# Early loads and own tiles for the first recurrence, four tiles for the last gates, and a 128 byte shift in a hybrid block kernel

## The chip, the core and the metric

The kernel runs on one core of a Trainium2 chip. The metric is the time of one execution in device microseconds (us); lower is better. Before the change it is 1393.91 us, the median of three runs (1393.51 to 1395.18).

## What is computed

One layer of a streaming encoder block works on 512 tokens of 2048 channels in float32. The normalised input is projected once, and the projection is split into parts:

- Branch A, a gated linear recurrence (HGRN2) with 8 heads of 128: `f = lb + (1 - lb) * sigmoid(a_f)`, `k = 1 - f`, `q = silu(a_q) / sqrt(128)`, and per head the state `S = diag(f) S + k v^T`, output `q S`. The output is normalised per head and multiplied by `silu(a_g)`.
- Branch B, sparse attention: an indexer scores all keys for every query and keeps the best 128, attention over these carries a relative position bias, and the output is multiplied by `silu(b_g)`.
- Merge: `sigmoid(m_a) * (y_a @ w_pa) + sigmoid(m_b) * (y_b @ w_pb)`, then `x + merged @ w_out`, then a last normalisation.

## The kernel before

**Products.** Every large product is made of three TensorE (PE) matmuls on operands split into a high and a low part (`split`, lines 71 to 73; `mm3`, line 75). Weights come from HBM in pieces of 512 KB through SyncE's (SP's) DMA queue into two raw buffers (`load`), are split by ScalarE (ACT) and VectorE (DVE) into one of three pairs `wh`, `wl` (`prep`, up to two pieces ahead), and are used by PE. SP issues in program order: a load that waits for its buffer holds up every DMA that was written behind it.

**Order.** `jobs` is a list of closures that is built by hand and run once. Inside a product job `pump()` is called at fixed places. A pump issues loads, sends out what the two `late` lists hold (stores, two pumps after they were noted) and lets each lane go one step. Lanes are generators: `hgrn` (the recurrences), `top` (the choice of keys), `att` (attention), `norm`, `misc`, `t5` (the bias table). So a lane's instructions stand in each engine's order between the blocks of a product.

**Stages**, in the order of time:

1. Start and first products (to 125 us).
2. Twelve pair units (125 to 584 us) make the gates and, first of all, `a_q` and `a_f` of heads 6 and 7 (stored in DRAM as `qf_d`; the gates as `gate_d`; `ckv_d` was stored before). A pair unit (`pair_unit`, line 1034) is a two by two product with seven multiplications (`PRODUCTS`, line 1024): 8 rounds of 7 x 2 x 3 = 42 matmuls with 256 moving columns. Stationary are the weights, split in pool `pairs` as `bh`, `bl` (three of the seven) and, as sums, in `wh`, `wl` (four of the seven); moving are the input `xh`, `xl` and its sums `sh`, `sl` in pool `sums`.
3. `close_pairs` frees these pools, `open_branches` (line 433) opens `values`, `shared` and `idx` and loads two small constants, and eight jobs of the indexer follow (584 to 645 us).
4. `end_index` (line 1130) frees the indexer's pools, opens `hgrn` (`R.h`) and `norms` (`R.i`), loads `ckv` and starts three lanes: the first recurrence `hgrn_gen(3)` (heads 6 and 7), `t5_gen` and `norm_gen`. Then `ai_job(3)` (line 650) makes the values `v` of these heads: 16 blocks of 12 matmuls with 256 moving columns, moving `wh`, `wl`, stationary `xh`, `xl`. For pair 3 it pumps after blocks 1, 2 and 3 of every four (12 pumps), for the others after 1 and 3 (8 pumps).
5. `af_aq(0)`, `open_att`, `ai_job(1)`, `af_aq(1)`, `ai_job(2)`, `uqkv(0)`, `af_aq(2)`, `uqkv(1)`: the other pairs' recurrence inputs, recurrences 0 to 2, attention.
6. `gate_job(44)` (line 1088) makes the last four gates with 512 moving columns, then `uqkv(2)`, the `w_pa` products and `uqkv(3)`.
7. `open_merge` (line 1217), the `w_pb` products and `merge_pair` (to 1221 us).
8. `out_job`: three pair units over `w_out` (1221 to 1340 us), this time with the merged tokens stationary (`mh`, `ml`, and their sums `so`) and the weights moving (`bh`, `bl` in a new pool `pairs` on the right side; `wh`, `wl`), then the last block and the final normalisation.

**The first recurrence.** `hgrn_gen(3)` loads `f` and `q` from `qf_d` into tiles of `R.h` in its first step (lines 701 to 703) and a gate (line 707); the second step makes `f`, `k` and `q` (lines 714 to 718); eight steps follow, one for each level `l`: `scores(l)` (small matmuls, tile `hl`), then `decay(l)` on DVE and POOL, which the next level's matmuls wait for. The others (`p` 0 to 2) find `f`, `k`, `q` in tiles that `af_evac` and `aq_evac` filled. `af_evac(p)` first runs to its end whatever is left of the recurrence before (`drain("hgrn")`), since the tiles `hf`, `hk` are shared.

**The last gates.** `gate_job` evicts four PSUM tiles with ACT into `gs`, a tile with two buffers in pool `values`, and each is stored to `gate_d` (lines 1090 to 1092).

**Places.** Pools are stacked from both ends of a partition, so a tile's first byte follows from the sizes. What matters below is that byte modulo 256. In the first twelve units: moving `xh` at 36,512, 52,896, ... and the sums from 106,144 on, all 160, apart from the sums of round 2 (`EVEN`), which a 64 byte gap puts at 224; stationary `bh` from 180,192 on and `wh` at 10,400 + 64, all 224. In the three units of `out_job`: moving `bh` from 208,864 on, 224, and `wh` at 10,400 + 192, which is 96 (in round 2 at 10,400, which is 160); stationary `mh` from 106,144 on and `so` at 52,896 and others, all 160. In `ai_job`: moving `wh` 96, stationary `xh` 160.

Of the kernel before, what the change touches and what calls it, by code (L numbers as in the profile page):

```python
# [26 lines left out]
F32 = mybir.dt.float32  # L27
FR = mybir.dt.float32r
AF = mybir.ActivationFunctionType
OP = mybir.AluOpType  # L30
# [4 lines left out]
T, D = 512, 2048  # L35
# [15 lines left out]
def hybrid_block(ctx, tc, x, norm_w, w_in, lb_table, gnorm_a, q_norm_w, kv_norm_w, w_uq,  # L51
# [3 lines left out]
    V, A, G, PE, SP = nc.vector, nc.scalar, nc.gpsimd, nc.tensor, nc.sync  # L55
# [45 lines left out]
    ckv_d = dram.tile([2, 128, T], F32, name="ckv_d")  # L101
    cq_d = dram.tile([4, 128, T], F32, name="cq_d")
    qf_d = dram.tile([2, 2, 128, T], F32, name="qf_d")
# [4 lines left out]
    def enter(name, side=None, space=None):  # L108
        cm = tc.tile_pool(name=name, bufs=1, side=side, reuse_waits="tile")
        pools[name] = (cm, cm.__enter__())  # L110
        return pools[name][1]
# [4 lines left out]
    R = SimpleNamespace()  # L116
# [83 lines left out]
    def drain(name):  # L200
        lane = lanes[name]
        while lane:
            for _ in lane[0]:
                pass
            lane.popleft()

    jobs, hg = [], {}
# [225 lines left out]
    def open_branches():  # L433
        R.v = enter("values")
        R.s = enter("shared")
        R.q = enter("idx", side="right")
        R.M = R.s.tile([128, 1280], F32, name="M")
        R.ckh = R.s.tile([128, 2, T], FR, name="ckh")
        R.ckl = R.s.tile([128, 2, T], FR, name="ckl")
        R.ident = R.s.tile([128, 128], F32, name="ident")  # L440
        R.levels = R.s.tile([128, 6, 32], U8, name="levels")
        SP.dma_start(R.ident, c_ident)
        lev = R.q.tile([128, 6, 32], F32, name="lev", tag="bf")
        SP.dma_start(lev, c_levels.rearrange("p (l t) -> p l t", l=6))
        G.tensor_copy(R.levels, lev)

    def t5_gen():
        rb = R.i.tile([128, H], F32, name="rb")
# [198 lines left out]

    def ai_job(p, places=(1, 3)):  # L650
        at = len(specs)
        c0 = 2048 + p * 256
        for k in range(0, NK, 4):
            specs.append(([(0, 256, w_in[k * 128:(k + 4) * 128, c0:c0 + 256])], 4, 256, MOVED))

        def run():
            ps = [mmp.tile([128, T], F32, name="acc") for _ in range(2)]
            for i in range(4):
                prep(at + i)
                wh, wl = halves.pop(at + i)  # L660
                for k in range(4):
                    kk = i * 4 + k
                    rh, rl = x_rhs(kk)
                    for t in range(4):
                        s = slice(t * 128, t * 128 + 128)
                        mm3(ps[t // 2][:, (t % 2) * 256:(t % 2) * 256 + 256], rh[:, s], rl[:, s],
                            wh[:, k, :], wl[:, k, :], kk == 0 and t % 2 == 0, kk == NK - 1)
                    if k in places:
                        pump()
            v = hg[p, "v"] = R.v.tile([128, 4, 256], F32, name="hv", bufs=2)  # L670
            for i in range(2):
                A.activation(v[:, 2 * i:2 * i + 2, :], ps[i].rearrange("p (t n) -> p t n", t=2), AF.Copy)

        jobs.append(run)

    def af_evac(p):
        def evac(c, ps):
            if c == 0:
                drain("hgrn")
                hg[p, "f"] = R.h.tile([128, 2, T], F32, name="hf")  # L680
                hg[p, "k"] = R.h.tile([128, 2, T], F32, name="hk")
            f, k, h = hg[p, "f"][:, c, :], hg[p, "k"][:, c, :], 2 * p + c
            A.activation(f, ps, AF.Sigmoid)
            V.tensor_scalar(f, f, oml[:, h:h + 1], lb[:, h:h + 1], op0=OP.mult, op1=OP.add)
            V.tensor_scalar(k, f, -1.0, 1.0, op0=OP.mult, op1=OP.add)
        return evac
# [10 lines left out]
        return evac  # L697

    def hgrn_gen(p):
        if p == 3:  # L700
            f, k, q = (R.h.tile([128, 2, T], F32, name=n) for n in ("hf", "hk", "hq"))
            SP.dma_start(f, qf_d[1].rearrange("f p t -> p f t"))
            SP.dma_start(q, qf_d[0].rearrange("f p t -> p f t"))
        else:
            q, k, f = hg[p, "q"], hg[p, "k"], hg[p, "f"]
        gate = R.h.tile([128, 2, T], F32, name="hg")
        SP.dma_start(gate, gate_d[2 * p:2 * p + 2].rearrange("f p t -> p f t"))
        S = R.h.tile([128, 8, 128], F32, name="hS")
# [1 line left out]
        G.memset(near, 0.0)  # L710
        G.memset(S, 0.0)
        qf, kf, tot = (a.rearrange("p c t -> p (c t)") for a in (q, k, f))
        yield
        if p == 3:
            for c in range(2):
                V.tensor_scalar(f[:, c], f[:, c], oml[:, 6 + c:7 + c], lb[:, 6 + c:7 + c], op0=OP.mult, op1=OP.add)
                V.tensor_scalar(k[:, c], f[:, c], -1.0, 1.0, op0=OP.mult, op1=OP.add)
            A.activation(q, q, AF.Copy, scale=128 ** -0.5)
            yield

        def scores(l, ps):

# [60 lines left out]
                                       tot[:, c * 4 + j:c * 4 + j + 1],  # L783
                                       pp[:, j * 128:(j + 1) * 128], op0=OP.mult, op1=OP.add)
        yield
        sq = R.h.tile([128, 2, T], F32, name="hk")
        zs = []
        o = R.h.tile([128, 2, T], F32, name="ho", tag="hf")
        for c in range(2):
            po = bank("ho")  # L790
            for j in range(4):
                sl = slice(j * 128, (j + 1) * 128)
                mm(po[:, sl], v[:, j, c * 128:(c + 1) * 128], S[:, 4 * c + j, :], j == 0, j == 0)
                if j:
                    mm(po[:, sl], st[:, c, j - 1, :], q[:, c, sl], False, True)
            A.activation(o[:, c], po, AF.Copy)
            A.activation(sq[:, c], po, AF.Square)
            yield
            zs.append((R.h.tile([128, T], FR, name="hzh", tag=("hkd", "hst")[c]),
                       R.h.tile([128, T], FR, name="hzl", tag=("hq", "hS")[c])))  # L800
            split(*zs[c], sq[:, c])
        yield
        for c in range(2):
# [8 lines left out]
            V.tensor_tensor(r, r, gate[:, c], op=OP.mult)  # L812
        yield
        for c in range(2):
            y = [R.h.tile([128, T], FR, name=f"hy{i}", tag=(("hkd", "hst"), ("hq", "hS"))[i][c]) for i in range(2)]
            split(*y, sq[:, c])
            for i in range(2):
                late[1].append(lambda y=y[i], i=i, h=2 * p + c: SP.dma_start(ya_d[i, h], y.bitcast(F32)))
# [268 lines left out]

    def gate_job(j0, after):
        def evac(c, ps):
            g = R.v.tile([128, T], F32, name="gs", bufs=2)  # L1090
            A.activation(g, ps, AF.Sigmoid)
            late[1].append(lambda: SP.dma_start(gate_d[j0 + c], g))

        feat_job(w_in, GATE_COL[j0], 4, NK, 2, x_rhs, evac, after=after)
# [35 lines left out]
    def end_index():  # L1130
        lanes["misc"].append(waiting.pop())
        drain("misc")
        leave("idx")
        leave("raws")
        R.h = enter("hgrn", side="right")
        R.i = enter("norms")
        R.ckv = R.i.tile([128, 2, T], F32, name="ckv")
        SP.dma_start(R.ckv, ckv_d.rearrange("f p t -> p f t"))
        lanes["hgrn"].append(hgrn_gen(3))
        lanes["t5"].append(t5_gen())  # L1140
        lanes["norm"].append(norm_gen(R.ckv, 2, c_kvw, R.ckh, R.ckl))
# [11 lines left out]
    def uqkv(p):  # L1153
        feat_job(w_uq, p * 256, 2, 4, 4, c_rhs, uq_evac(p), place=RANK,
                 before=None if p else (lambda: drain("top")))
        ukv_job(p)

    jobs.append(end_index)
    ai_job(3, (1, 2, 3))
    lane("top", top_gen)  # L1160
    af_aq(0)
    jobs.append(open_att)
    ai_job(1)
    af_aq(1)
    ai_job(2)
    uqkv(0)
    af_aq(2)
    uqkv(1)
# [127 lines left out]
    def out_job():  # L1296
# [7 lines left out]
        def run():  # L1304
# [3 lines left out]
            def block_evac(c0):  # L1308
                def evac(ps):
                    p1, p2, p6, p7, p5, p3, p4 = ps  # L1310
                    c = R.v0.tile([128, 4, 256], F32, name="hv")
                    one, u2 = c[:, 0:2, :], c[:, 2:4, :]
                    u3 = R.g.tile([128, 2, 256], F32, name="u3")

                    def part(t0, f0, in0, in1, op):
                        V.tensor_tensor(two[t0 // 2][:, :, c0 + f0:c0 + f0 + 256], in0, in1, op=op)

                    A.activation(one, p1, AF.Copy)
                    V.tensor_tensor(u2, p6, one, op=OP.add)
                    part(0, 256, p2, one, OP.add)  # L1320
                    V.tensor_tensor(u3, p7, u2, op=OP.add)
                    V.tensor_tensor(u2, p5, u2, op=OP.subtract)
                    part(2, 0, p5, u3, OP.subtract)
                    part(0, 0, p3, u2, OP.add)
                    part(2, 256, p4, u3, OP.add)
                return evac
# [83 lines left out]
            for t in range(4):  # L1410
# [16 lines left out]
                o, f = os[t], out2[t * 128:(t + 1) * 128]  # L1427
# [67 lines left out]
```

## Time and profile before

| what | us |
|---|---|
| median of three runs | 1393.91 |
| the profiled execution | 1394.53 |
| its span, first to last instruction | 1392.7 |
| PE busy | 1363.5 (98%) |
| DVE busy | 1064.6 (76%) |
| ACT busy | 624.1 (45%) |
| POOL busy | 84.2 (6%) |

The profile is of one execution. Busy time counts the records of an engine; matmuls are pipelined, so a record is longer than the step from its start to the start of the next one, and that step is what a matmul costs in a stream. PEclk is the granted TensorE clock as a share of 2.4 GHz. A wait is the idle time of an engine before an instruction, put down to what came last.

### The profile page before, as it was taken

Reading aid. Unit: us, or ns where it says so; the run is one execution under the profiler, and the core shown is the slowest. Engines: PE = TensorE matmul, PEld = TensorE weight load, DVE = VectorE, ACT = ScalarE, POOL = GpSimd, SP = SyncE. Lnnn points to the kernel's source line nnn. Section 1 sums busy time; section 2 is a strip of 40 time slices with the busy share of each in tenths; the row PEclk is TensorE's granted clock in tenths of the full one; section 3 lists DMA queues with packets and bytes.
Section 4 is the critical chain, followed back from the end, with each engine's and each line's share of the span. In section 5 each row is a group of like instructions: output and inputs, shape, how many; then the busy total and the mean of one; then the engine's idle time right before and its main releaser. Section 6 shows DMA issues by size and latency. Waiting matters only on the chain. (4 is left out here: it accounts for less than half of the span.)

```text
span 1392.7 us, 26397 instructions
## 1 busy us (share of the span) xinstructions
PE 1363.5 (98%) x10796; PEld 1256.5 (90%) x10796; DVE 1064.6 (76%) x1745; ACT 624.1 (45%) x985; POOL 84.2 (6%) x85
## 2 busy tenths in 40 slices
PE   8999999999999999998899999999999999999997
PEld 7888999999999999997789889888788888899996
DVE  7786789988888888676768698666465558898856
ACT  6544544545444444364251424543543334454434
POOL 2100000000000000000302012112010100000000
PEclk9999999999999999999999999999999999999999
DMA  6344345544444444523333242345484656643554
GB/s 203 91 109 147 92 142 162 167 137 138 148 141 136 141 129 116 167 83 123 108 116 98 61 138 88 118 134 163 151 288 159 218 166 218 205 152 107 166 192 171
DMA packets 141834, 201.59 MB, mean 145 GB/s; under 512 B 10209, under 2 KB 83602, under 8 KB 141586
## 3 DMA queue, kind: packets, MB, share of 16 engines
q1 hardware_dynamic: 140322, 198.53, 45.7%
q8 instruction: 84, 1.38, 0.4%
q10 hardware_dynamic: 1392, 1.39, 0.3%
q14 instruction: 36, 0.29, 0.1%
HBM read 165.80 MB, written 34.09 MB: 144 GB/s over the span
## 5 line engine op out<-in xcount | busy, mean ns | idle before, releaser
L150 ACT ACTIVATE bh<-wr 128x768 fp32r<-128x768 f32 x120 | 101.5, 846 | 214.7 <-issue 115.0
L72 ACT ACTIVATE wh<-wr 128x1024 fp32r<-128x1024 f32 (+1 forms) x112 | 116.6, 1042 | 180.2 <-PE acc L77 61.1
L73 DVE TENSOR_TENSOR wl<-wr,wh 128x1024 fp32r<-128x1024 f32 (+1 forms) x112 | 137.5, 1229 | 61.7 <-ACT wh L72 61.7
L152 ACT ACTIVATE wh<-sv 128x512 fp32r<-128x512 f32 x240 | 141.8, 622 | 75.5 <-DVE sv L145 57.6
L78 PE MATMUL pp<-sh,wl 128*128 128x256 f32 x576 | 159.5, 277 | 0.0
L76 PE MATMUL pp<-sh,wh 128*128 128x256 f32 x576 | 159.5, 277 | 0.0
L77 PE MATMUL pp<-sl,wh 128*128 128x256 f32 x576 | 159.4, 277 | 0.0
L153 DVE TENSOR_TENSOR bl<-wr,bh 128x768 fp32r<-128x768 f32 x120 | 114.7, 956 | 50.9 <-ACT bh L150 50.5
L154 DVE TENSOR_TENSOR wl<-sv,wh 128x1024 fp32r<-128x1024 f32 x120 | 146.7, 1223 | 7.3 <-ACT wh L152 1.1
L76 PE MATMUL acc<-xh,wh 128*128 128x512 f32 x368 | 146.9, 399 | 0.0
L78 PE MATMUL acc<-xh,wl 128*128 128x512 f32 x368 | 143.5, 390 | 0.0
L77 PE MATMUL acc<-xl,wh 128*128 128x512 f32 x368 | 143.4, 390 | 0.0
L77 PEld LDWEIGHTS pp<-sl,wh 128*128 128x128 f32 x576 | 108.3, 188 | 0.0
L78 PEld LDWEIGHTS pp<-sh,wl 128*128 128x128 f32 x576 | 108.3, 188 | 0.0
L76 PEld LDWEIGHTS pp<-sh,wh 128*128 128x128 f32 x576 | 108.3, 188 | 0.0
L76 PE MATMUL pp<-xh,bh 128*128 128x256 f32 x384 | 106.0, 276 | 0.0
L78 PE MATMUL pp<-xh,bl 128*128 128x256 f32 x384 | 106.0, 276 | 0.0
L77 PE MATMUL pp<-xl,bh 128*128 128x256 f32 x384 | 106.0, 276 | 0.0
L76 PE MATMUL acc<-yh,wh 128*128 128x512 f32 x256 | 100.0, 391 | 0.0
L78 PE MATMUL acc<-yh,wl 128*128 128x512 f32 x256 | 99.7, 389 | 0.0
L77 PE MATMUL acc<-yl,wh 128*128 128x512 f32 x256 | 99.7, 389 | 0.0
L145 DVE TENSOR_TENSOR sv<-wr 128x512 f32<-128x512 f32 x120 | 82.4, 687 | 7.4 <-DMA wr<-in_w_in_dram 4.9
(386 smaller groups left out, 3653.4 us busy)
## 6 DMA issues: line engine op xcount, KB each, us to landing
wr<-in_w_in_dram SPq DMA_DIRECT2D x144, 512.0 KB, 3.7
wr<-in_w_out_dram SPq DMA_DIRECT2D x32, 512.0 KB, 4.3
mg<-gate_d SPq DMA_DIRECT2D x48, 256.0 KB, 4.3
gate_d<-c SPq DMA_DIRECT2D x44, 256.0 KB, 5.1
wr<-in_w_pa_dram SPq DMA_DIRECT2D x16, 512.0 KB, 5.9
wr<-in_w_pb_dram SPq DMA_DIRECT2D x16, 512.0 KB, 3.8
wr<-in_w_in_dram SPq DMA_DIRECT2D x20, 256.0 KB, 3.1
x<-in_x_dram SPq DMA_DIRECT2D x8, 512.0 KB, 6.4
```

Source lines behind the costliest of these rows:

```text
L72: A.activation(hi, src, AF.Copy)
L73: V.tensor_tensor(lo, src, hi.bitcast(F32), op=OP.subtract)
L76: PE.matmul(ps, lh, rh, start=first, stop=False, skip_group_check=True)
L77: PE.matmul(ps, lh, rl, start=False, stop=False, skip_group_check=True)
L78: PE.matmul(ps, ll, rh, start=False, stop=last, skip_group_check=True)
L145: V.tensor_tensor(sv[:, 0:2, :], b[:, 1:3, :], b[:, 0:1, :].to_broadcast([128, 2, 256]), op=OP.add)
L150: A.activation(bh, b[:, 1:4, :], AF.Copy)
L152: A.activation(vh[:, i:i + 2, :], sv[:, i:i + 2, :], AF.Copy)
L153: V.tensor_tensor(bl, b[:, 1:4, :], bh.bitcast(F32), op=OP.subtract)
L154: V.tensor_tensor(vl, sv, vh.bitcast(F32), op=OP.subtract)
```

## The change

- `open_branches` opens `norms` and loads there, in its last lines, `f` and `q` of the first recurrence and `ckv`, with a tile for `k` beside them; `end_index` no longer does so.
- `hgrn_gen(3)` takes these tiles. Its first step now also makes `f`, `k` (one DVE instruction for two) and `q`; a helper `place` keeps later tiles of recurrence 3 that reuse `hf`, `hk`, `hq` in the new tiles.
- `ai_job(3)` pumps 8 times like the others, and `af_evac(0)` no longer drains the recurrence.
- `open_att` (which drains `norm` and `t5`, frees `norms` and opens `att`) moves from behind `af_aq(0)` to behind `ai_job(2)`.
- `gs` gets four buffers, in pool `us` (`R.u`), which lies where `hgrn` lay.
- `u3`, a tile in the right hand pool `pairs` of `out_job`, is 544 columns wide instead of 512, of which 512 are used. The pool starts 128 bytes lower: `bh` from 208,736 on, 96 modulo 256.

```diff
@@ open_branches
         G.tensor_copy(R.levels, lev)
+        R.i = enter("norms")
+        R.last = [R.i.tile([128, 2, T], F32, name=n) for n in ("hf", "hk", "hq")]
+        R.ckv = R.i.tile([128, 2, T], F32, name="ckv")
+        for t, src in ((R.last[0], qf_d[1]), (R.last[2], qf_d[0]), (R.ckv, ckv_d)):
+            SP.dma_start(t, src.rearrange("f p t -> p f t"))
@@ ai_job
-    def ai_job(p, places=(1, 3)):
+    def ai_job(p):
...
-                    if k in places:
+                    if k % 2 == 1:
                         pump()
@@ af_evac
-                drain("hgrn")
+                if p:
+                    drain("hgrn")
@@ hgrn_gen
-        if p == 3:
-            f, k, q = (R.h.tile([128, 2, T], F32, name=n) for n in ("hf", "hk", "hq"))
-            SP.dma_start(f, qf_d[1].rearrange("f p t -> p f t"))
-            SP.dma_start(q, qf_d[0].rearrange("f p t -> p f t"))
-        else:
-            q, k, f = hg[p, "q"], hg[p, "k"], hg[p, "f"]
+        f, k, q = R.last if p == 3 else (hg[p, n] for n in "fkq")
+
+        def place(shape, dtype, name, tag):
+            pool = R.i if p == 3 and tag in ("hf", "hk", "hq") else R.h
+            return pool.tile(shape, dtype, name=name, tag=tag)
+
...
-        yield
         if p == 3:
             for c in range(2):
                 V.tensor_scalar(f[:, c], f[:, c], oml[:, 6 + c:7 + c], lb[:, 6 + c:7 + c], op0=OP.mult, op1=OP.add)
-                V.tensor_scalar(k[:, c], f[:, c], -1.0, 1.0, op0=OP.mult, op1=OP.add)
+            V.tensor_scalar(k, f, -1.0, 1.0, op0=OP.mult, op1=OP.add)
             A.activation(q, q, AF.Copy, scale=128 ** -0.5)
-            yield
+        yield
@@ gate_job
-            g = R.v.tile([128, T], F32, name="gs", bufs=2)
+            g = R.u.tile([128, T], F32, name="gs", bufs=4)
@@ end_index
-        R.i = enter("norms")
-        R.ckv = R.i.tile([128, 2, T], F32, name="ckv")
-        SP.dma_start(R.ckv, ckv_d.rearrange("f p t -> p f t"))
@@ the list of jobs
-    ai_job(3, (1, 2, 3))
+    ai_job(3)
     lane("top", top_gen)
     af_aq(0)
-    jobs.append(open_att)
     ai_job(1)
     af_aq(1)
     ai_job(2)
+    jobs.append(open_att)
     uqkv(0)
@@ out_job, block_evac
-                    u3 = R.g.tile([128, 2, 256], F32, name="u3")
+                    u3 = R.g.tile([128, 544], F32, name="u3")[:, :512].rearrange("p (f n) -> p f n", f=2)
```

## Rows read from the trace of the kernel before

**Rows 1.** Waits of PE, whole span: who, for whom, us, times, longest.

```profile
PE hl L81 <- ACT hq L718: 5.0, 1, 5.0
PE acc L76 <- ACT gs L1091: 2.5, 1, 2.5
```

**Rows 2.** Busy time by stretch: us, engines (instructions), clock, DMA share, GB/s.

```profile
652.00:656.00 4.00, 0.13 (x8) 0.13 (x12) 1.86 (x4) 1.24 (x2) 0.00 (x0) 0.81 1.04 384
656.00:662.00 6.00, 6.00 (x86) 4.72 (x86) 3.85 (x6) 2.39 (x3) 0.00 (x0) 0.56 0.03 8
...
1006.00:1008.50 2.50, 0.09 (x1) 0.00 (x0) 0.00 (x0) 0.60 (x1) 0.00 (x0) 1.00 0.49 188
1008.50:1013.00 4.50, 4.46 (x13) 3.51 (x14) 3.07 (x5) 4.47 (x7) 0.00 (x0) 0.62 0.00 1
```

**Rows 3.** Waits of all engines between 620 and 700 us.

```profile
ACT hq L718 <- DMA hq<-qf_d: 6.9, 1, 6.9
...
DVE hf L716 <- DMA hf<-qf_d: 4.7, 1, 4.7
```

**Rows 4.** Timeline of SP's queue between 560 and 700 us.

```profile
566.73 15.81 SPq L128 DMA_DIRECT2D wr<-in_w_qidx_dram  x4
...
590.53 19.63 SPq L128 DMA_DIRECT2D wr<-in_w_qidx_dram  x4
...
648.11 0.37 SPq L128 DMA_DIRECT2D wr<-in_w_in_dram  x1
648.53 0.50 SPq L702 DMA_DIRECT2D hf<-qf_d  x1
649.08 0.46 SPq L703 DMA_DIRECT2D hq<-qf_d  x1
```

**Rows 5.** Busy time of two whole ai jobs: PE, PEld, DVE, ACT, POOL, clock.

```profile
645.20:689.60 44.40, 35.85 (x640) 31.80 (x640) 31.65 (x50) 13.76 (x19) 12.09 (x11) 0.92 0.32 103
740.40:769.10 28.70, 28.34 (x609) 27.01 (x607) 26.55 (x47) 5.23 (x6) 9.02 (x6) 1.00 0.28 79
```

**Rows 6.** Timeline of PE: small products between the blocks of ai job 3.

```profile
656.75 1.47 PE L460 MATMUL t<-oh,rb 128*8 128x384 f32 x2
...
663.24 0.49 PE L81 MATMUL ns<-sumh,ones_r 128*128 128x512 f32 x1
...
678.17 1.12 PE L473 MATMUL t<-bf,flip 128*128 128x512 f32 x2
...
685.04 1.15 PE L81 MATMUL hl<-hq,hk 128*64 128x64 f32 x16
...
687.60 0.82 PE L768 MATMUL hkt<-ident,hk 128*128 128x128 f32 x6
```

**Rows 7.** Timeline of ACT at the last gates.

```profile
1007.89 1.23 ACT L1091 ACTIVATE gs<-acc 128x512 f32<-128x512 f32 x2 [10.51 <-DMA gate_d<-gs]
```

**Rows 8.** Timeline of SP at the last gates: stores of recurrence 2.

```profile
993.20 2.88 SPq L818 DMA_DIRECT2D ya_d<-hy  x4
```

**Rows 9.** DMAs of tile hy between 980 and 1010 us.

```profile
DMA to landing us min/median/max: 3.8/4.2/4.5
```

**Rows 10.** Busy time of tile pp alone, by stretch (PE first).

```profile
125.10:584.40 459.30, 459.27 (x4032) 459.27 (x4031) 51.23 (x81) 6.95 (x12) 1.00 0.46 138
1221.10:1340.00 118.90, 118.90 (x1008) 118.87 (x1007) 11.08 (x18) 1.74 (x3) 1.00 0.48 156
...
125.10:135.00 9.90, 9.88 (x84) 9.87 (x84) 0.00 (x0) 0.00 (x0) 1.00 0.47 132
...
140.00:163.80 23.80, 23.80 (x212) 23.80 (x211) 2.09 (x4) 0.58 (x1) 1.00 0.38 111
163.80:202.10 38.30, 38.30 (x339) 38.30 (x338) 4.52 (x8) 0.58 (x1) 1.00 0.46 139
```

**Rows 11.** Timeline of PE: first and last of ai job 3's first 48 matmuls.

```profile
645.26 0.28 PE L76 MATMUL acc<-wh,xh 128*128 128x256 f32 x1
...
650.60 0.28 PE L78 MATMUL acc<-wh,xl 128*128 128x256 f32 x1
```

More of the change, by code (lines that the diff above doesn't have):

```diff
@@ L785, in hgrn_gen @@
         yield
-        sq = R.h.tile([128, 2, T], F32, name="hk")
+        sq = place([128, 2, T], F32, "hk", "hk")
         zs = []
-        o = R.h.tile([128, 2, T], F32, name="ho", tag="hf")
+        o = place([128, 2, T], F32, "ho", "hf")
         for c in range(2):
@@ L798, in hgrn_gen @@
             yield
-            zs.append((R.h.tile([128, T], FR, name="hzh", tag=("hkd", "hst")[c]),
-                       R.h.tile([128, T], FR, name="hzl", tag=("hq", "hS")[c])))
+            zs.append((place([128, T], FR, "hzh", ("hkd", "hst")[c]), place([128, T], FR, "hzl", ("hq", "hS")[c])))
             split(*zs[c], sq[:, c])
@@ L814, in hgrn_gen @@
         for c in range(2):
-            y = [R.h.tile([128, T], FR, name=f"hy{i}", tag=(("hkd", "hst"), ("hq", "hS"))[i][c]) for i in range(2)]
+            y = [place([128, T], FR, f"hy{i}", (("hkd", "hst"), ("hq", "hS"))[i][c]) for i in range(2)]
             split(*y, sq[:, c])
```

## The prediction

> **What bounds the kernel now.** I read the page first: TensorE (PE) is busy for 98% of the span, every other engine far less. So PE's order is the path nearly everywhere, and the question for each part of the change is how much PE time it gives back or takes. Second, the waits of PE: two lie where the change works, 5.0 us of a score matmul for the scaled `q` of the first recurrence and 2.5 us of a gate matmul for an eviction into `gs` [rows 1]. Third, the stretches around them, for what an idle PE costs afterwards: in the 6.0 us behind the first wait PE is busy throughout, yet the granted clock is 0.56 of 2.4 GHz, that is nearly all of it at the 1.2 GHz level; in the 4.5 us behind the second it is 0.62 [rows 2]. Fourth, the step from one `pp` matmul to the next in the pair units, which is not the same in the two groups of units [rows 10].
>
> **First recurrence: the cause.** SP issues the loads of `f` and `q` at 648.5 and 649.1, behind a weight load [rows 4]; ACT and DVE then sit 6.9 and 4.7 us for them [rows 3]. Ai job 3 does its first 48 matmuls from 645.26 to 650.60 [rows 11] and then has a level's scores next in PE's order, with 144 matmuls of its own behind them that need nothing of the recurrence. The new code issues the two loads in `open_branches`, some 60 us earlier, so they have landed when the lane starts. The first pump now makes `f`, `k`, `q`. In the old code these were the 4 DVE and 2 ACT instructions that took 1.86 and 1.24 us [rows 2]. The first pump comes after 24 of the 48 matmuls, at about 648.0 by rows 11, the level's scores at 650.7: 2.7 us for 1.86. The one `k` instruction for two saves at most one fixed cost, hidden: 0.
>
> **Its size, two ways.** (a) Ai job 1 has the same 192 matmuls and the eight pumps that ai job 3 now gets, with seven levels between them: 28.7 us at clock 1.00, against 44.4 at 0.92 for job 3 [rows 5]. Of that difference the following is work and not loss, and goes on existing: the eighth level 1.15, `hkt` 0.82, the two `t` pairs of 1.12, the pair at 1.47 which ran at the low clock (half, 0.74), and the `ns` pair (0.49 for one, 0.7 estimated for both) [rows 6]: 5.7 in all. The loss is 44.4 - 28.7 - 5.7 = 10.0. (b) The wait is 5.0 [rows 1]; the 6.0 us at 0.56 lose 6.0 x 0.44 = 2.6 [rows 2]; what is left of the window is 44.4 - 35.85 = 8.55 idle [rows 5], 5.0 of it the wait, so some 3.5 more, small gaps before levels whose decay on DVE and POOL was not ready, because 12 pumps put levels closer than 8 do. Some of this belongs to any such job (28.7 - 28.34 = 0.4): 5.0 + 2.6 + 3.1 = 10.7. I take **10.5**. Ends: 5.0 if only the wait goes and DVE then sets the pace (31.65 us of work on DVE in what would be a 34 us window [rows 5]), and 11.8 if the extra work, counted by starts and not by overlapping durations, is 3.9 instead of 5.7. I stay near the middle because job 1 itself runs without loss with DVE busy 26.55 of 28.7, and the moved last level takes DVE work out of job 3. That level then stands in `af_aq(0)`, where its 1.15 us of PE work was counted above; without the drain it is spread over pumps.
>
> **What the early loads are put in front of.** Three DMAs of 512 KB each, at about 0.5 us of issue (0.50, 0.46 [rows 4]), now stand in SP's queue ahead of the second four indexer weight pieces of 590.53. The first four pieces were issued by 566.73 + 15.81 = 582.5 [rows 4] and serve the first four of eight jobs, which take 60.8/8 = 7.6 us each; so the fifth piece is needed at 584.4 + 4 x 7.6 = 614.8. Behind the loads it is issued at about 592. From the issue of `hq`, done at 649.5, to the matmul at 655.9 that used it were 6.4 us, arithmetic included [rows 1, 4, 11]; the 1.5 MB ahead of the piece adds about 4 (at the 384 GB/s of rows 2). So it is ready at about 603, and the cover is some 12 us: 0. The new tiles lie where `sums` lay, last read by PE at 584.4 [rows 10], so SP doesn't wait there. The loads behind the old place (`hg`, the bias table) come 1 to 2 us earlier: 0. Moving `open_att` costs 0: what it drains has long run out, and its tiles are first used in `uqkv(0)`.
>
> **Last gates.** The third `gs` eviction waited 10.51 us, until 1007.89, for a store of a buffer to land [rows 7]; PE stood from 1006.0 to 1008.5 [rows 2]. With four tiles no eviction waits for a store of `gs`. Gain 2.5 of wait and 4.5 x (1 - 0.62) = 1.7 of clock: **4.2**. Ends: 2.5 (the clock falls anyhow) and 4.3. The new places lie over tiles of recurrence 2 from which `hy` is stored: four stores issued from 993.20 on over 2.88 us [rows 8], each landing within 4.5 [rows 9], the last by 1000.6. Evictions that wait for these then take 4 x 0.62 and are done by about 1003.1, 2.9 us before PE needs the third bank at 1006.0. So ACT may still wait, PE not. Late next is nothing that I find: the stores behind in SP's queue go out earlier as well.
>
> **128 bytes.** In the first twelve units a `pp` matmul costs 459.3/4032 = 113.9 ns, in the three of `out_job` 118.9/1008 = 118.0 [rows 10], with the same shape at clock 1.00. Stationary minus moving, modulo 256, is +64 in the first group (224 - 160; 0 in round 2), and in `out_job` +64 for `wh` but -64 for `bh` (160 - 224). After the change `bh` is at 96, so +64, as everywhere in the first group. Ai job's matmuls at +64 (160 - 96) step at 5.34/47 = 113.6 [rows 11]. But the offset alone doesn't make the fast step: the first 84 matmuls of the first unit cost 9.90/84 = 117.9 at +64, the 42 of round 2 119 (135.00 to 140.00), the 212 behind it 23.80/212 = 112.3, and a later whole unit takes 38.30 [rows 10]. So I expect the first unit of `out_job` like the very first one (9.90 + 5.0 + 23.80 = 38.7, from 125.1 to 163.8) and two of 38.25: 115.2 instead of 118.9, a gain of **3.7**. Ends: 4.5 if all ran at the fast step (1008 x 113.6 = 114.5), and a loss of 1.1 if all cost the 119 ns of that round 2, whose offset is 0 (1008 x 119 = 120.0).
>
> Against it stands a rule of the Trainium skill ("TensorE: Matmul & The Clock Gate", section "Step-by-step: what each phase is for"): PE has two independent read ports, so loading the next weights takes no read bandwidth from the running matmul. By it the two places would not matter and this term would be 0. The rows show 113 and 118 ns for one shape, which the rule doesn't tell apart; they don't show that the place is the cause.
>
> **Sum.** 10.5 + 4.2 + 3.7 = 18.4. The profiled execution took 1394.5, 0.6 over the median of 1393.91: 1394.5 - 18.4 = 1376.1, and 1375.5 as a median.
>
> **Rivals.**
> (1) The shift is worth nothing, because the step hangs on something else that differs (weights moving instead of stationary, other pools): 14.7 remain, 1379.2. For it: both steps occur at the same offset in the first unit. Against it: eleven units in a row hold the fast step. Chance 0.14.
> (2) DVE or POOL becomes the bound in ai job 3: only the wait of 5.0 goes there; 5.0 + 4.2 + 3.7 = 12.9, so 1381.0. For: 31.65 of DVE in that job; against: job 1 at 28.7. Chance 0.11.
> (3) The `gs` evictions wait for `hy` stores long enough that PE waits as before: 14.2 remain, 1379.7. It needs stores 3 us later than those of rows 9. Chance 0.04.
> (4) Slower: SP, which issues in order, stands at the early loads because their places are still in use, and holds the fifth indexer piece. With a cover of some 12 us, a stand of X costs PE X - 12; above X = 12 + 18.4 = 30 the kernel is slower than before. If the places came free only with the indexer's end (645), X is 55 and PE idles 43: about 1418. Against: `sums` is closed at 584. Chance 0.02.
>
> **The numbers.** Forecast 0.69, the rivals 0.14, 0.11, 0.04, 0.02. The range takes the good ends (11.8 + 4.3 + 4.5 = 20.6, to 1373.3, and 1.3 for the scatter of the runs) and reaches over rivals 1 to 3: 1372.0 to 1381.5. A measurement of this kernel can tell about 0.2%, 2.8 us, from no change; all cases but (4) lie over 12 us below: faster 0.96, the rest split between (4) and bad ends together.
>
> **What would show it.** No wait of PE for `hq` L718 or for `gs`; `hf` and `hq` issued at about 590, ai job 3 in some 34 us at clock 1.00; if it is 37 to 39 with DVE over 90% busy, rival 2 holds. A `gs` eviction may wait for `ya_d<-hy`; PE after it must not. Tile `pp` in `out_job` over 115 us, its units 38.7, 38.3, 38.3; 118.9 means rival 1, near 120 the bad end. An indexer matmul waiting for `wr` near 615 would be rival 4. The prediction is wrong if the median is over 1381.5, or if a new wait of over 1 us stands in the stages between.

## The result, and the profile after

The changed kernel takes 1380.16 us, the median of four runs (1379.67 to 1381.48), against 1394.55 for the kernel before on the same chip (four runs). The ratio is 0.9898, 95% interval 0.9881 to 0.9915. The forecast was 1375.5 with a range of 1372.0 to 1381.5: the time lies in the range, 4.7 us above the forecast, and the gain is 14.4 us where the terms had 18.4.

The profiled execution took 1380.42 us; that of before 1394.53. Where the 14.1 us between them lie, by the start of the first matmul of each stage (for the gates, of their last one):

| stretch | before | after | change | predicted |
|---|---|---|---|---|
| start to the first pair unit | 125.12 | 126.19 | +1.06 | 0 |
| pair units and indexer, to ai job 3 | 520.13 | 520.11 | 0 | 0 |
| ai job 3 and `af_aq(0)` | 95.17 | 88.24 | -6.9 | -10.5 |
| ai job 1 to the last matmul of the last gates | 257.78 | 257.58 | -0.2 | 0 |
| from there, over `uqkv(2)`, to the first `w_pa` product | 17.63 | 13.35 | -4.3 | -4.2 |
| to the pair units of `out_job` | 205.25 | 205.24 | 0 | 0 |
| these three units | 118.92 | 115.16 | -3.8 | -3.7 |
| the rest | 52.7 | 52.7 | 0 | 0 |

The first line is chance: in the profiles of this study that stretch is 124.6 to 126.2 us long, whatever the kernel. Two terms came out as worked out, one did not.

**The first recurrence.** The waits of PE in ai job 3 and `af_aq(0)`, in the changed kernel (640 to 740 us; who, for whom, us, times, longest):

```profile
PE hl L81 <- DVE tot L749: 1.6, 1, 1.6
PE acc L78 <- DVE wl L73: 1.5, 1, 1.5
PE hp L81 <- ACT hkd L774: 0.3, 1, 0.3
```

The wait of 5.0 for `hq` [rows 1] is gone, but waits of 1.6 and 1.5 us stand here. The first of these stood in the kernel before too (1.75, below); the second, in `af_aq(0)`, is new. The busy time by stretch, changed kernel: ai job 3, then `af_aq(0)`, then the stretch that held the first wait and its aftermath (us, PE, PEld, DVE, ACT, POOL, clock, DMA share, GB/s):

```profile
646.30:678.00 31.70, 29.99 (x617) 27.80 (x615) 24.67 (x37) 12.21 (x16) 7.94 (x6) 1.00 0.37 111
678.00:734.50 56.50, 54.68 (x266) 43.86 (x265) 36.23 (x85) 23.36 (x32) 3.42 (x4) 1.00 0.36 109
650.00:662.00 12.00, 12.00 (x270) 10.82 (x270) 9.69 (x14) 3.07 (x4) 3.37 (x2) 1.00 0.50 157
```

and `af_aq(0)` in the kernel before:

```profile
689.70:740.40 50.70, 50.70 (x242) 41.99 (x241) 33.19 (x78) 21.82 (x29) 0.96 (x1) 1.00 0.45 135
```

Ai job 3 went from 44.4 [rows 5] to 31.7, and the clock of the stretch from 0.56 to 1.00 [rows 2]. The forecast had some 34 for it, with all its small products; some of these now stand in `af_aq(0)`. That stage, where PE had been busy all the time, grew by 5.8: by this work, and by 1.8 us of waits.

SP's queue in the changed kernel shows the early loads and the indexer pieces behind them:

```profile
591.29 0.49 SPq L450 DMA_DIRECT2D hf<-qf_d  x1
591.82 0.47 SPq L450 DMA_DIRECT2D hq<-qf_d  x1
592.33 0.47 SPq L450 DMA_DIRECT2D ckv<-ckv_d  x1
593.21 3.32 SPq L128 DMA_DIRECT2D wr<-in_w_qidx_dram  x2
```

SP doesn't wait at the loads, and the indexer's jobs take 60.8 us as before.

**The last gates.** ACT's timeline, changed kernel:

```profile
990.21 0.60 ACT L1095 ACTIVATE gs<-acc 128x512 f32<-128x512 f32 x1
993.46 1.58 ACT L1095 ACTIVATE gs<-acc 128x512 f32<-128x512 f32 x3 [2.65 <-DMA ya_d<-hy]
```

Beside it PE's stretch over these evictions:

```profile
992.00:1002.00 10.00, 10.00 (x49) 8.35 (x48) 3.90 (x5) 4.82 (x8) 0.00 (x0) 1.00 0.75 249
```

An eviction now waits 2.65 us for a store of recurrence 2 whose place it takes, instead of 10.51 for its own [rows 7], and PE is busy throughout at clock 1.00.

**The shift.** Tile `pp` alone, changed kernel: the three units, the first 84 matmuls, the first unit from its round 3 on, and the second unit:

```profile
1210.70:1325.90 115.20, 115.19 (x1008) 115.12 (x1007) 10.92 (x18) 1.74 (x3) 1.00 0.50 160
1210.70:1220.60 9.90, 9.88 (x84) 9.88 (x84) 0.00 (x0) 0.00 (x0) 1.00 0.73 237
1225.60:1249.40 23.80, 23.80 (x213) 23.80 (x212) 1.88 (x3) 0.58 (x1) 1.00 0.47 143
1249.40:1287.70 38.30, 38.30 (x339) 38.30 (x338) 4.58 (x8) 0.58 (x1) 1.00 0.37 112
```

These are, window by window, the times of the first two of the twelve units [rows 10]: 9.90, 23.80, 38.30.

### The profile page after: what moved, and what is told of

Its sections match the earlier page's. It is cut to its first block, busy times and chain, and to the rows that moved or that the text cites. A ratio compares the mean times of both kernels' runs of the same rounds, so it can differ in the third digit from the quotient of the medians.

```text
span 1378.6 us, 26386 instructions
## 1 busy us (share of the span) xinstructions
PE 1357.1 (98%) x10796; PEld 1250.5 (91%) x10796; DVE 1062.2 (77%) x1744; ACT 625.0 (45%) x986; POOL 82.6 (6%) x85
## 4 chain that ended last, share of the span: by engine, by line
PE 86%; DVE 9%; ACT 2%; issue 1%; DMA 1%; POOL 0%; ACTq 0%; SPq 0%; DVEq 0%; POOLq 0%
PE pp L77 14%; PE pp L76 14%; PE pp L78 14%; PE acc L76 12%; PE acc L78 12%; PE acc L77 12%; DVE wl L73 1%; PE acc L81 1%; PE hl L81 1%; DVE M L648 1%; DVE m L647 1%; PE ho L81 1%; DVE hq L744 1%; PE sc L78 1%; PE sc L76 1%
```

## The experiments

**Each part alone.** The kernel before with one part of the change: the first recurrence (the changed kernel with `gs` and `u3` as before), the gates, the shift.

```diff
# only_gates, on the kernel before
-            g = R.v.tile([128, T], F32, name="gs", bufs=2)
+            g = R.u.tile([128, T], F32, name="gs", bufs=4)
# only_shift, on the kernel before
-                    u3 = R.g.tile([128, 2, 256], F32, name="u3")
+                    u3 = R.g.tile([128, 544], F32, name="u3")[:, :512].rearrange("p (f n) -> p f n", f=2)
```

> The first recurrence's part alone (early loads, eight pumps, no drain, later pool), with the old gs and the old u3. Theory from the two traces: ai job 3 and af_aq(0) together take 88.2 us instead of 95.2, so 6.9 us less than before, some 1387.5; the waits that are left (1.6 us for the decay of a level, 1.5 us for the weights' low part in af_aq(0)) stand in this kernel too. Rival (the prediction's own size): 10.5 us, 1384, if the missing 3.6 us in the changed kernel came from the other parts of the change or from the one profiled run. Lower end: 5.0 us.

> Four gs tiles in the later pool alone. Theory: the wait of 2.5 us of PE and the 1.7 us at the low clock behind it go, 4.2 to 4.5 us less than before, some 1389.5; the first gs evictions wait for the stores of hy, PE does not. Rival: only the wait goes, 2.5 us, with the clock still down; or nothing, when PE waits for the late evictions.

> u3 of 544 columns alone. Theory (place modulo 256): tile pp in the last three units takes 115.2 us instead of 118.9, 3.7 us less than before, some 1390.2, and nothing else moves. Rival: in the changed kernel the fast step came from what stands ahead of these units, then 118.9 here and no gain.

Measured, each against the kernel before at 1393.87 us, the gains by the ratio: the first recurrence 1386.38, ratio 0.9948 (0.9935 to 0.9960), 7.2 us less; the gates 1390.69, 0.9977 (0.9969 to 0.9986), 3.2 less; the shift 1389.60, 0.9974 (0.9963 to 0.9985), 3.6 less. The ratios multiply to 0.9899, against 0.9898 for the whole change: within the intervals the parts add, and none hides another. The edits inside the first part (early loads, one step less, no drain, the later `open_att`) were run only together. The stretches of ai job 3 and `af_aq(0)` in the first of them are 31.70 and 56.50 us again, so the missing 3.6 us are a property of this part. For the gates, the times alone leave room for "only the wait goes"; the profile of that kernel has the stage at 13.34 us against 17.63, 4.3 less. The profiled execution of it, 1392.21, is one of the longer ones: the indexer, which this edit doesn't touch, takes 62.3 us there instead of 60.8, with a clock of 0.83 in a stretch that has 1.00 in the kernel before:

```profile
590.00:600.00 10.00, 9.18 (x42) 8.56 (x43) 6.69 (x11) 4.74 (x10) 0.62 (x1) 0.83 0.54 169
```

For the shift, tile `pp` in the three units:

```profile
1219.60:1334.80 115.20, 115.19 (x1008) 115.12 (x1007) 10.94 (x18) 1.74 (x3) 1.00 0.49 161
```

**Twelve pumps again.** The changed kernel with the pumps of before in ai job 3.

```diff
-    def ai_job(p):
+    def ai_job(p, places=(1, 3)):
...
-                    if k % 2 == 1:
+                    if k in places:
...
-    ai_job(3)
+    ai_job(3, (1, 2, 3))
```

> The changed kernel with twelve pumps in ai job 3 instead of eight. Theory A: four steps that moved into af_aq(0) make its new wait for the weights' low part (1.5 us) and its slow matmul blocks (1.2 us); with them back in ai job 3 af_aq(0) takes 50.7 us again less what is left of the lane, and the total is 1 to 3 us under the changed kernel, 1377 to 1379. The wait of 1.6 us for a level stays, since it is the norm lane's DVE work that stands ahead of that decay. Theory B (as the prediction had it): levels that stand closer wait for each other's decay; ai job 3 then shows waits of 2 to 3 us more and the total is 1 to 3 us over the changed kernel, 1381 to 1383.

Measured: 1380.83 us (1380.04 to 1382.60), ratio 0.9909 (0.9895 to 0.9922): not to be told from the changed kernel. Its stretches of ai job 3 and `af_aq(0)`:

```profile
645.30:683.70 38.40, 33.55 (x640) 30.20 (x640) 31.08 (x48) 13.64 (x19) 11.15 (x8) 1.00 0.30 92
683.70:734.40 50.70, 50.70 (x242) 41.98 (x241) 33.09 (x77) 21.85 (x29) 0.95 (x1) 1.00 0.45 136
```

and its waits of PE in ai job 3:

```profile
PE hl L81 <- DVE tot L749: 2.3, 2, 1.6
PE t L465 <- DMA oh<-in_buckets_dram: 1.1, 1, 1.1
PE hl L81 <- DVE hq L744: 0.9, 1, 0.9
PE hl L81 <- DVE hk L722: 0.4, 1, 0.4
PE hl L81 <- POOL hk L746: 0.2, 1, 0.2
```

Each theory is right about one half, and the time lies between their ranges. With twelve pumps `af_aq(0)` has no wait and takes 50.7 again (A), but ai job 3 has 4.9 us of waits where it had 1.7 (B), 1.1 of them for a load of the bias table and not for a level; together 89.1 against 88.2. So eight pumps took 3.1 us of waits out of ai job 3, as much as the sum gave them, but `af_aq(0)` got 1.8 of waits back, and by the two profiles they were worth about 1 us. The wait of 1.6 is there with both.

**Whose wait is it?** DVE's timeline ahead of that wait, changed kernel, and the matmul that waits:

```profile
668.14 0.73 DVE L581 SCALAR_TENSOR_TENSOR nt<-ckv,cols,rr 128x512 f32<-128x512 f32 x1
669.57 0.82 DVE L73 TENSOR_TENSOR ckl<-nt,ckh 128x512 fp32r<-128x512 f32 x1 [0.70 <-ACT ckh L72]
670.31 0.74 DVE L581 SCALAR_TENSOR_TENSOR nt<-ckv,cols,rr 128x512 f32<-128x512 f32 x1
671.75 0.69 DVE L73 TENSOR_TENSOR ckl<-nt,ckh 128x512 fp32r<-128x512 f32 x1 [0.70 <-ACT ckh L72]
672.36 0.69 DVE L744 TENSOR_TENSOR hq<-hq,tot 128x512 f32<-128x512 f32 x1
672.96 0.22 DVE L749 TENSOR_TENSOR tot<-tot 128x64 f32<-128x64 f32 x1
```

```profile
673.19 0.75 PE L81 MATMUL hl<-hq,hk 128*32 128x32 f32 x64 [1.59 <-DVE tot L749]
```

The norm lane's last step, 4.3 us with two halts for ACT, stands in DVE's order between two levels. The kernel before has the same four instructions and, behind them,

```profile
674.31 0.75 PE L81 MATMUL hl<-hq,hk 128*32 128x32 f32 x64 [1.75 <-DVE hq L739]
```

To test it, the norm lane was started elsewhere: in `open_branches` (ckv is loaded there now), after the fourth indexer job, and behind ai job 1 (this one on top of the kernel with the bias table's stores on SP, below).

```diff
# norm_early: in open_branches, behind the loads; norm_mid: a job behind the fourth of the indexer's
# norm_late: a job behind ai_job(1); each takes it out of end_index
+        lanes["norm"].append(norm_gen(R.ckv, 2, c_kvw, R.ckh, R.ckl))
...
-        lanes["norm"].append(norm_gen(R.ckv, 2, c_kvw, R.ckh, R.ckl))
```

> The changed kernel with the norm lane started in open_branches, where ckv is loaded now, so that its DVE and ACT work falls into the indexer's jobs. Theory: the wait of 1.6 us of PE for a level in ai job 3 comes from the norm lane's instructions, of which the low part waits on DVE for ACT, ahead of that level's decay; it goes, and the total is 1.5 to 2 us under the changed kernel, some 1378.3. Rival (DVE is simply short in ai job 3, or the pumps too close): the wait shows up at another level and the total is that of the changed kernel, 1380.2.

> The changed kernel with the norm lane started after the fourth of the indexer's eight jobs, when ckv has landed. Theory: the losses of the earlier start came from ACT, which works in order and stood at the norm lane's first instruction until ckv had landed; now none of that, ai job 3 is 2 to 2.5 us shorter as it was with the earlier start, the indexer's jobs no more than 1 us longer, total 1 to 2.5 us under the changed kernel, 1377.7 to 1379.2. Rival: the indexer has no room on ACT and DVE for the lane at all, its matmuls wait for relu and qih, and the total is over the changed kernel, 1381 to 1386.

> The changed kernel with the bias table's stores on SP, and the norm lane started behind ai job 1, so that it runs in af_aq(1), where DVE is busy for 39 of 50 us and ACT for 21. Theory: the norm lane's work ahead of a level's decay makes the wait of 1.6 us in ai job 3; there it goes, ai job 3 is 2 to 2.5 us shorter, af_aq(1) longer only by the lane's 0.6 us of small matmuls that move there too; total 1.5 to 2.5 us under the kernel with the stores on SP alone, some 1375. Rival: af_aq(1) has no room either, PE waits there for weights or for the lane, total 1377 to 1379.

Measured: 1391.59 us (ratio 0.9982, 0.9973 to 0.9991), 1382.89 (0.9924, 0.9910 to 0.9938) and 1382.45 (0.9917, 0.9903 to 0.9930). The first and the last are slower than the kernels that they were built on (0.9898 and, below, 0.9884); the middle one by intervals that just overlap, but on top of the stores on SP the same edit takes 1380.13 us where that kernel takes 1377.38 (below). Ai job 3 in the three of them:

```profile
659.00:688.20 29.20, 29.20 (x615) 27.18 (x613) 22.30 (x31) 5.68 (x7) 8.88 (x6) 1.00 0.40 120
```

```profile
652.50:681.60 29.10, 29.10 (x613) 27.09 (x612) 22.23 (x31) 5.67 (x7) 8.83 (x6) 1.00 0.39 120
```

```profile
646.90:676.10 29.20, 29.20 (x614) 27.18 (x613) 22.31 (x31) 7.39 (x10) 8.83 (x6) 1.00 0.39 120
```

In all three PE has no idle time left there and the job takes 2.5 us less: the wait was the norm lane's. (Its 2.4 us of DVE work leave the job with it, 24.67 to 22.3; no run kept the work and changed only its place in the order.) And all three lose more elsewhere. The indexer's jobs take 74.1 and 67.7 us instead of 60.8; ai job 1 and `af_aq(1)` together take 86.4 in the latest start instead of 79.7 in the kernel that it was built on. PE's waits there, early (two lines), middle and late:

```profile
PE sc L76 <- ACT qih L72: 6.5, 2, 5.6
PE sc L76 <- ACT relu L629: 3.5, 2, 3.3
...
PE sc L76 <- ACT relu L628: 3.4, 2, 3.3
...
PE acc L78 <- DVE wl L73: 2.8, 1, 2.8
```

In the earliest start ACT stands 8.9 us at the lane's first instruction until ckv has landed, and the `qih` that PE waits for comes behind it; the clock of 600 to 620 us is 0.84:

```profile
598.92 1.15 ACT L566 ACTIVATE nsq<-ckv 128x512 f32<-128x512 f32 x2 [8.88 <-DMA ckv<-ckv_d]
```

So the first theory holds for the wait and fails for the total, where even its rival (1380.2) was far too low. The rival of the middle start was right (1381 to 1386). That of the late one named the right wait, but its 1377 to 1379 fell short of 1382.45. The place in ai job 3 is the cheapest of the four.

**The other wait.** ACT's timeline in `af_aq(0)`, changed kernel:

```profile
711.88 1.06 ACT L812 ACTIVATE hk<-hk 128x1024 f32<-128x1024 f32 x1
717.40 0.37 ACTq L481 DMA_DIRECT2D bh_d<-nt  x1
717.80 1.28 ACT L689 ACT_TABLE_LOAD   x1 [4.86 <-DVE nt L480]
719.09 0.60 ACT L689 ACTIVATE hf<-acc 128x512 f32<-128x512 f32 x1
719.59 1.14 ACT L72 ACTIVATE hy<-hk 128x512 fp32r<-128x512 f32 x2
720.63 2.00 ACT L72 ACTIVATE wh<-wr 128x1024 fp32r<-128x1024 f32 x2
```

ACT stands 4.86 us at the issue of the bias table's last store, for a copy that DVE makes behind the recurrence's normalisation; the weights are split after that. In the kernel before it was issued at 705.7, ahead of that normalisation (714.0 to 716.8), and so it is at 699.7 in the changed kernel with twelve pumps (normalisation from 707.9 on): with eight pumps it falls behind. The edit gives the stores to SP, two pumps later:

```diff
-            A.dma_start(bh_d[h:h + 2].rearrange("h p c -> p h c"), e)
+            late[1].append(lambda h=h, e=e: SP.dma_start(bh_d[h:h + 2].rearrange("h p c -> p h c"), e))
```

> The changed kernel with the bias table's four stores issued by SP, two pumps later, instead of by ACT. Theory: in af_aq(0) ACT stood 4.9 us at the issue of the last of these stores, for a copy that DVE had behind the recurrence's normalisation, and so split the next weights late; PE's wait of 1.5 us for their low part goes, total 1 to 2 us under the changed kernel, 1378.2 to 1379.2. Rival: the recurrence's own tail on DVE and ACT makes the weights late, the wait stays within 0.5 us, total 1380.2.

> Both edits. If both theories hold the gains add: 2 to 4 us under the changed kernel, 1376 to 1378, near the 1375.5 that was predicted for it. If one of the rivals holds, what the other kernel alone gives.

Measured: 1377.38 us (1377.27 to 1378.01), ratio 0.9884 (0.9870 to 0.9897); together with the norm lane in the indexer 1380.13, 0.9907 (0.9893 to 0.9920). Stores on SP, ai job 3 and `af_aq(0)`:

```profile
645.80:677.60 31.80, 30.02 (x616) 27.82 (x615) 24.70 (x37) 13.90 (x19) 7.92 (x6) 1.00 0.36 110
677.60:731.80 54.20, 54.20 (x267) 44.18 (x266) 37.97 (x86) 22.49 (x30) 3.91 (x4) 1.00 0.39 117
```

PE has no wait left in `af_aq(0)`, and the stretch is 2.3 us shorter than in the changed kernel, a little more than was expected. This kernel has the lowest median of the study, but the interval of its ratio overlaps that of the changed kernel (0.9881 to 0.9915): the stage shows the gain, the times don't yet. The two edits together missed their 1376 to 1378: ai job 3 takes 29.2 and `af_aq(0)` 54.1, so both gains are there, but the indexer's stretch is 6 us longer.

**The shift.** The changed kernel with `u3` 576 and 528 columns wide, and without the other place of `wh` in round 2.

```diff
# shift256
-                    u3 = R.g.tile([128, 544], F32, name="u3")[:, :512].rearrange("p (f n) -> p f n", f=2)
+                    u3 = R.g.tile([128, 576], F32, name="u3")[:, :512].rearrange("p (f n) -> p f n", f=2)
# shift64: 528
# no_even
-            pair_specs(w_out, [cb * 512, cb * 512 + 256], NK // 2, even=EVEN)
+            pair_specs(w_out, [cb * 512, cb * 512 + 256], NK // 2)
```

> The changed kernel with u3 576 columns wide: the pool starts 256 bytes lower than before the change, so bh is at 224 modulo 256 again, stationary minus moving -64. Theory (place modulo 256): tile pp in the last three units takes 118.9 us as before the change, all rounds near 117.8 ns, 3.7 us more than the changed kernel. Rival (a lower pool or a hole behind u3 does it): 115.2.

> The changed kernel with u3 528 columns wide: bh at 160 modulo 256, stationary minus moving 0 for bh, +64 for wh. Theory (only +64 for all gives the fast step): 118.7 to 121 us for tile pp in the last three units. Rival (only -64 is bad): 115.2.

> The changed kernel without the other place of wh in round 2 of the last three units: +64 in every round. Theory (the step has two states at +64, and a round at another offset is what leads from the slow to the fast one): all rounds of all three units stay at 117.8 ns, 118.8 us for tile pp, 3.6 us more than the changed kernel. Rival (the place alone, whatever round 2 does): the units are as fast or faster than in the changed kernel, 114.5 to 115.2 us.

One run each: 1383.54, 1382.37 and 1383.77 us; what is compared is the stage. Tile `pp` in the three units, 256 bytes lower (offset -64 for `bh`):

```profile
1210.10:1329.00 118.90, 118.90 (x1008) 118.88 (x1007) 11.06 (x18) 1.74 (x3) 1.00 0.48 156
```

64 bytes lower (offset 0 for `bh`):

```profile
1210.20:1327.80 117.60, 117.59 (x1008) 117.57 (x1007) 11.00 (x18) 1.73 (x3) 1.00 0.48 157
```

no other place in round 2 (+64 everywhere), the three units and the second of them:

```profile
1210.50:1329.20 118.70, 118.70 (x1008) 118.67 (x1007) 11.07 (x18) 1.74 (x3) 1.00 0.48 156
...
1250.10:1289.60 39.50, 39.50 (x338) 39.50 (x337) 4.29 (x8) 0.58 (x1) 1.00 0.34 107
```

A pool that is lower by 256 bytes gives back all of the gain, so it is not a hole or a lower pool. The pool 0, 64, 128 and 256 bytes lower gave 118.9, 117.6, 115.2 and 118.9 us: the place modulo 256 fits this, and no other multiple of 256 was run. Offset 0 gives 117.6, a little under the range of its theory, and far from its rival's 115.2. Its timeline splits this. In the last round of a unit the mean step from one matmul to the next is 117.9 ns among those with `bh`, at offset 0, and 114.8 among those with `wh`, at +64; in the kernel before, with `bh` at -64, it is 118.1 and 117.4. And at the good offset everywhere nothing is gained when round 2 is like the others.

## Why the prediction was right or wrong

- **The time and the signs.** The time lies in the range, but the range was drawn to reach over rivals 1 to 3, so the time alone doesn't tell the forecast from these; the stages do. And one of the prediction's own two signs of being wrong has come: "a new wait of over 1 us stands in the stages between". It is PE's 1.5 us for `wl` in `af_aq(0)`.
- **Last gates, right.** 4.2 predicted, 4.3 in the stage's profile, 3.2 (2.0 to 4.3) in the timed part alone. The new wait for `hy` came about where it was put: it ends at 993.46, and PE did not feel it, so the rival of late stores falls.
- **The 128 bytes, right in size.** 3.7 predicted from units one and two of the first group, 3.8 in the stage, 3.6 (2.1 to 5.2) alone. The prediction said that the offset alone doesn't make the fast step; without round 2's other place it doesn't. (Its 112.3 ns for the fast step divides by 212 records, two of which the window's edges cut; by the 210 matmuls it is 113.3, and no term of the sum uses it.) That `out_job` has such a round it didn't name as a condition, and there it was lucky. The rule of the Trainium skill that was weighed there ("TensorE: Matmul & The Clock Gate", "Step-by-step: what each phase is for": the next weights' load takes no read bandwidth from the running matmul) was read as a gain of nothing for any place. The traces don't agree with that reading: 118.9, 117.6 and 115.2 us for one shape at three places say that places matter here, and nothing in the runs says by which port.
- **Early loads, right.** No wait of SP at the loads, none of PE for `wr` in the indexer; rival (4) falls.
- **First recurrence, right in kind and mis-sized: 10.5 for 6.9.** Against the 10.7 of way (b), 3.8 us are missing, in four places.
  - The largest, 1.8, is a term put at nothing: the steps that eight pumps leave over were priced in `af_aq(0)` at their PE work alone, "where its 1.15 us of PE work was counted above". There they delayed the lanes, and PE waits 1.5 for weights and 0.3 for `hkd` in a stage that had no wait.
  - The third summand, "some 3.5 more, small gaps before levels ... because 12 pumps put levels closer than 8 do", of which 3.1 was counted as gone, lost 1.8 (idle time beside the wait of 5.0: 3.55 before, 1.71 after), so 1.3 are missing. Way (a) has the same step, as ai job 1 was taken for ai job 3 with eight pumps. Ai job 1 has no norm lane; ai job 3 has, and 1.75 us of those gaps were its doing and stayed (1.59).
  - The clock's term, put at 2.6, is 2.3: in the run with twelve pumps the same 640 matmuls of ai job 3 keep PE busy for 33.55 us instead of 35.85.
  - PE's busy time over both stages is 84.67, 0.4 more than with twelve pumps (84.25). With the stores on SP it is 84.22, so this went with the waits of `af_aq(0)`.
- **Rivals (1), (2) and (3)** gave 1379.2, 1381.0 and 1379.7, all nearer to the result than the forecast, but not for their reasons. The shift is worth its 3.8; DVE is busy 24.67 of 31.7 us in ai job 3, not over 90%; and PE doesn't wait for the `gs` evictions. What DVE and ACT were late for had other lanes' instructions ahead of it.

## What to carry to other kernels

When small steps of several lanes stand in one engine's order, a gap before one lane's matmul can be the work of another lane (here 1.6 us): look at the instructions ahead of the late one on its engine before you credit the gap to a spacing you are about to change. A sister stage is a good measure only if the same lanes run in it, and steps that a stage no longer holds must be priced where they go, with what stands behind them there: a store issued by the engine that also splits weights held the splits up for 4.86 us. A matmul stream's step can hang on operand places, here by their bytes modulo 256; compare the steps of equal shapes between stages, and between the first and later rounds of one stage.

## What the runs showed of the hardware that was not expected

The step of the same matmul, at the same places and clock 1.00, has two values, 117.9 ns (9.90 us for 84) and about 113 (23.80 for 210; a unit of 336 with its slower round 2 takes 38.30), and which one it has depends on what ran before. At offset +64 in every round the slow one stood for all 1008 matmuls of `out_job` (118.70 us). With one round that has part of its operands at another offset the fast one came behind that round and stayed for the units behind it. In the first group the fast one follows such a round too, but there no run took the round's other place away. With `bh` at -64 the same round did not bring it (118.90). What in the engine holds this is open; no run here looked into it.
